# Up-projection sums in PSUM on copies written by ScalarE, a new order of its seven products, and down-projection in halves of 352 columns

## The chip, the cores and the metric

The kernel runs on one core of a Trainium2 chip. Its time is device microseconds, the median of several executions. The core has a matrix engine (TensorE, in the profile PE, with its weight loads as PEld), a vector engine (VectorE, DVE), a scalar engine (ScalarE, ACT), GpSimd (POOL) and SyncE (SP), which here only issues DMA transfers. Matmul results land in PSUM, eight banks of 512 fp32 columns; DVE and ACT read and write PSUM, everything else lies in SBUF.

## The reference

One layer of a streaming encoder for 2048 prompt tokens and 64 sample tokens (2112 columns in all), followed by a final RMSNorm. The part that the change touches is the gated MLP with a causal depthwise convolution of width 3:

```python
h2 = rmsnorm(x, g2) * (1 + sc2) + sh2
up = h2 @ w_up                          # 1024 -> 2 * 2816
upp = jnp.concatenate([conv_buf.astype(up.dtype), up], 1)
conv = b_conv + sum(w_conv[j] * upp[:, j:j + T] for j in range(CONV_W))
a, g = jnp.split(conv, 2, -1)
x = x + gt2 * ((jax.nn.silu(g) * a) @ w_down)   # 2816 -> 1024
```

All inputs and outputs are fp32. Before this part come the adaLN modulation, a pooling mixer, an mLSTM with four heads and the output projection.

## The kernel before

**Precision.** Every large product is made of three passes over operands split into a high and a low part (`PASSES`, L436: high by high, high by low, low by high). ACT writes the high part (L384), DVE the low part (L387); for weights this happens as they come in from memory. A few weights are kept in DRAM already split and are loaded whole.

**The MLP's tiling.** The 2112 tokens are three groups of 704 columns (`FT`), each two halves of 352 (`FH`). The 2816 channels are 22 tiles of 128 (`f`), each with a value tile (a) and a gate tile (g); the pair of both is an object `Pair`. A group is worked in four parts of 5, 5, 6 and 6 pairs (`PARTS`): first the up-projection of the part's pairs, then the down-projection of the part's channels, whose result is added to `x3`.

**Seven products.** For one pair, the two output tiles by two token halves, and the 1024 inputs cut in two, make a 2 by 2 block product, which is done with seven products instead of eight (`product`, L1537: 4 blocks of 128 inputs by 3 passes, 12 matmuls of 352 columns). The names say which sums of the input go in: B11, B21, T2, T3, B22, T1, T4 (`BN`). The weights are two quarters of `w_up`, a third (loaded for T4), and four sums of quarters (`wsum`, made earlier by DVE). The sums of the moving input, tiles `hx`, are made in the order of `BN`: for the first group by ACT and DVE just before the MLP begins (`sums_of`, L728, with L743 and L750), for the others during the group before, through DRAM (`prepare`, `reload`).

The output is put together from the products: the a tile's first half is B11 + B21, its second half B11 + T2 + T1 + B22; the g tile's second half is B11 + T2 + T1 + T3, its first half B11 + T2 + T3 + T4. In `Pair.products` (L1566) PE accumulates in three PSUM banks: b1 takes B11, T2, T1; b2 takes B21 and, after it is read, B22; b3 takes T3 and T4. ACT copies b1 to SBUF after B11 (`s1`, L1582), after T2 (`u2`, L1591) and after T1 (`u4`, L1606), and DVE adds a bank and a copy four times: L1595 for a's first half, and through `plus` (L1551) `sum_a`, `sum_g1`, `sum_g0`. PE's order in a pair is B11, B21, the T4 of the pair before, T2, T3, B22, T1.

**After the sums.** `conv_scale` (ACT, L1525) and two `conv_tap` (DVE, L1530) make the convolution of a and g, `silu` (ACT, L1637) and `gate` (DVE, L1641) the gated value, `split_hi` (ACT, L1646) and `split_lo` (DVE, L1651) its two parts in a tile `av`. These steps are written between the products of the next two pairs.

**Down-projection.** `down` (L1814) multiplies the `av` tiles by `w_down`, for 8 output tiles n; a group of columns (`secs`) has a bank of its own, so one n takes two banks: columns 0 to 448 and 448 to 704 (`ENDS`). The first three n are begun before the last pair is ready, and that pair's remaining steps (`todo`) are done between their matmuls. `down_end` (L1836) adds the banks to `x3` on DVE (L1841). In the last part of the last group the two column groups are worked one after the other, each for n = 3 to 7, so that the output of the first can leave early.

**What sets the order.** In the MLP the kernel's own text is the order of PE, ACT, DVE and POOL (`manual_schedule`); there is no planner between. Each engine takes its instructions in that order. Six PSUM banks go round for `mm_ps()`. The loads are a list, `stream` (L326 to L328 for the up-projection), in the order in which products use them; SP issues them up to seven units ahead (`ahead`, L1493), at most seven weight tiles being live, and the splits of at most four units ahead are written in front of each product (`pump`, L394). Background work (`tick`) of the next group is written between matmuls.

Of the kernel before, what the change touches and what calls it, by code (L numbers as in the profile page):

```python
# [11 lines left out]
AF = mybir.ActivationFunctionType  # L12
ALU = mybir.AluOpType
# [13 lines left out]
FH = FT // 2  # L27
NFG = NTOK // FT
NE = 3
EB = 1  # L30
ENDS = ((0, 448), (448, 704))
PARTS = ((0, 5), (5, 10), (10, 16), (16, 22))
EPS = 1e-6
HD = 128
# [24 lines left out]
def tile_layer(ctx: ExitStack, tc: tile.TileContext, xT, vecs, cst, rst, w_mod, w_ada, w_qkou, w_v, w_pool,  # L59
               w_out, w_up, w_down, st_C, st_pool, yT, o_pool, o_C, o_m, o_conv):  # L60
    nc = tc.nc
    act, dve, pool, pe = nc.scalar, nc.vector, nc.gpsimd, nc.tensor
# [8 lines left out]
    def bank(nm, shape=(P, 512)):  # L71
        q = turn[nm]
        q.append(q.pop(0))
        return q[-1].tile(list(shape), F32, tag="bank", name=nm)
# [3 lines left out]
    def mm_ps():  # L78
        return bank("mm")
# [12 lines left out]
    def scr():  # L92
        return sp.tile([P, TMAX], F32, tag="scr", name="scr")
# [4 lines left out]
    def tick(i=0):  # L98
        q = bg[i]
        while q:  # L100
            try:
                next(q[0])
                return
            except StopIteration:
                q.pop(0)
# [35 lines left out]
    half = cp.tile([P, 8 + 32], F32, tag="half", name="half")[:, :8]  # L141
# [4 lines left out]
    ones_r = cp.tile([P, P], F32R, tag="ones_r", name="ones_r")  # L146
# [102 lines left out]
    for g in range(NG):  # L249
        o = Grp()  # L250
# [20 lines left out]
    stream = []  # L271
# [30 lines left out]
    WS2, WS4, WS3, WS1 = range(4)  # L302
    KEPT = (WS2, WS1)

    def down_order(nf):

        out = [(n, k) for n in range(NE - 1) for k in range(nf - 2)] + [(n, nf - 2) for n in range(NE - 1)]
        out += [(NE - 1, k) for k in range(nf - 1)] + [(n, nf - 1) for n in range(NE)]
        return out + [(n, k) for n in range(NE, KD) for k in range(nf)]

    def up_unit(f, i):
        return w_up[NF + f if i > 1 else f, :, (i % 2) * 512:(i % 2) * 512 + 512]
# [4 lines left out]
    def sum_unit(g, f, i):  # L317
        if i not in KEPT:
            return (wsum[f, :, i], 512, INSIDE, None)
        kept = wsplit[f, KEPT.index(i)]  # L320
        return (kept, 512, WHOLE, None) if g else (wsum[f, :, i], 512, INSIDE, kept)

    for g in range(NFG):
        for (f0, f1_) in PARTS:
            late = []
            for f in range(f0, f1_):  # L326
                stream += [(up_unit(f, 0), 512), (up_unit(f, 1), 512)] + late
                stream += [sum_unit(g, f, i) for i in (WS2, WS3, WS4, WS1)]  # L328
                late = [(up_unit(f, 3), 512)]
            order = down_order(f1_ - f0)  # L330
            ends = g == NFG - 1 and f1_ == NF
            seen = set()
            for i, (n, k) in enumerate(order):
                if i == f1_ - f0 - 2:
                    stream += late
                c = f0 + k // 4 * 4
                if k % 4 == 0 or (n, c) not in seen:
                    seen.add((n, c))
                    d = min(c + 4, f1_)
                    stream.append((w_down[n, :, c * P:d * P], (d - c) * P, OUT, None, ends and n >= NE))  # L340
# [53 lines left out]
    def pump():  # L394

        while True:
            for i, u in enumerate(pend[:ahead[1]]):
                if u.w is not None or live[0] < ahead[2] or u.stays:
                    work_out(u, 2 if i < ahead[1] - ahead[3] else 1)
            if (pos[0] >= len(stream) or len(pend) >= ahead[0] or live[0] >= ahead[2]  # L400
                    or sum(u.w is None for u in pend) >= RB
                    or pos[0] < n_att and sum(u.w is not None for u in pend) >= WB - 2):
                break
            issue()
# [3 lines left out]
    def get_unit():  # L408
        if not pend:
            issue()  # L410
        u = pend.pop(0)
        work_out(u)
        if spare:

            owed.append(u)
        else:
            keep(u)
        return u.w

    def settle(n=0):  # L420
        while len(owed) > n:
            keep(owed.pop(0))
# [203 lines left out]
    for g in range(NFG):  # L626
        o = Grp()
# [6 lines left out]
    B = []  # L634
# [182 lines left out]
    if True:  # L817
# [399 lines left out]
        def proj(o, h):  # L1217
            W = Row()
            ps = [mm_ps() for _ in o.blks]
            gemm(ps, W, h, o)  # L1220
            return ps
# [14 lines left out]
        ends = []  # L1236
# [174 lines left out]
        for o in groups:  # L1411
# [16 lines left out]
            if o.g == 0:  # L1428
                t = scr()
# [11 lines left out]
            for hd in range(NH):  # L1441
# [3 lines left out]
                if o.g == 0 and hd == 0:  # L1445
                    xs = rows_of(groups[1])
                    t = scr()
# [21 lines left out]
            for gi in U_ORDER:  # L1469
                ps = proj(o, h)  # L1470
# [62 lines left out]
    def spans(o, half):  # L1533

        return [(pa, pb, a + 2 + 2 * s) for (i, pa, pb, a, b, s) in o.pieces if i == half]

    def product(ps, Bo, nm, first):  # L1537
        pump()
        settle()
        U = get_unit()  # L1540
        for kc in range(4):
            for pi, (a, b) in enumerate(PASSES):
                pe.matmul(ps[:, :FH], U[:, a, kc * P:(kc + 1) * P], Bo.at(nm, kc, b),  # L1543
                          start=(first and kc == 0 and pi == 0), stop=(kc == 3 and pi == 2), skip_group_check=not first)
            if kc % 2:
                tick(0)
        live[0] -= 1

    def plus(o, half, ext, u, ps):
        for (a, b, d) in spans(o, half):  # L1550
            dve.tensor_tensor(out=ext[:, d:d + b - a], in0=ps[:, a:b], in1=u[:, a:b], op=ALU.add)  # L1551

    def half_tile(nm):
        return f1.tile([P, FH], F32, tag=nm, name=nm)

    class Pair:
# [9 lines left out]
        def products(self, old):  # L1566


            o, Bo, f = self.o, self.Bo, self.f
            self.before = old  # L1570
            older = old and old.before
            b1, b2 = self.b1, self.b4 = mm_ps(), mm_ps()

            def rest(*steps):
                for pair, step in steps:
                    if pair:
                        step(pair)
            rest((old, Pair.copy_u4), (older, Pair.gate))
            product(b1, Bo, "B11", True)
            rest((old, Pair.sum_g1), (old, Pair.sum_a))  # L1580
            self.s1 = half_tile("s1")
            act.activation(self.s1, b1[:, :FH], AF.Copy)  # L1582
            rest((older, Pair.split_hi))
            product(b2, Bo, "B21", True)
            rest((old, Pair.scale_a), (older, Pair.split_lo))
            if old:
                old.last_product()
            rest((old, Pair.taps_a), (old, Pair.sum_g0))
            product(b1, Bo, "T2", False)
            self.u2 = half_tile("u2")  # L1590
            act.activation(self.u2, b1[:, :FH], AF.Copy)  # L1591
            rest((old, Pair.scale_g))
            self.ea = ext_tile(o, f, "a")
            for (a, b, d) in spans(o, 0):
                dve.tensor_tensor(out=self.ea[:, d:d + b - a], in0=b2[:, a:b], in1=self.s1[:, a:b], op=ALU.add)  # L1595
            self.b3 = mm_ps()
            product(self.b3, Bo, "T3", True)
            rest((old, Pair.taps_g))
            tick(1)
            product(self.b4, Bo, "B22", True)  # L1600
            rest((old, Pair.silu))
            product(b1, Bo, "T1", False)

        def copy_u4(self):
            self.u4 = half_tile("u4")
            act.activation(self.u4, self.b1[:, :FH], AF.Copy)  # L1606

        def sum_a(self):
            plus(self.o, 1, self.ea, self.u4, self.b4)

        def scale_a(self):
            self.ta = conv_scale(self.o, self.f, self.ea, "a")

        def sum_g1(self):
            self.eg = ext_tile(self.o, NF + self.f, "g")
            plus(self.o, 1, self.eg, self.u4, self.b3)

        def sum_g0(self):
            plus(self.o, 0, self.eg, self.u2, self.b3)

        def scale_g(self):
            self.tg = conv_scale(self.o, NF + self.f, self.eg, "g")
# [77 lines left out]
    late, YLATE = [], 6  # L1700
# [84 lines left out]
    ET = mybir.EngineType  # L1785
    fctx.enter_context(tc.manual_schedule(engines={ET.PE, ET.Activation, ET.DVE, ET.Pool}))
    x3, ssum = [], None
    for o in fgroups:
        Bo = B[o.g]
        for pi, (f0, f1_) in enumerate(PARTS):  # L1790
            nf = f1_ - f0
            lastp = pi == len(PARTS) - 1
            ends = o.last and lastp
            av = [None] * nf
            pair = None
            for f in range(f0, f1_):
                old, pair = pair, Pair(o, Bo, f, f - f0, av)
# [57 lines left out]
                if ends:  # L1855
                    act.activation(x3[n][:, lo:hi], x3[n][:, lo:hi], AF.Copy, scale=V[:, V_GF + n:V_GF + n + 1])

            both = ENDS
            Ws = [Row() for _ in range(NE)]
            pss = []  # L1860

            old = pair.before
            pair.copy_u4()
            todo.extend([both_of(pair.sum_g1, old.gate), both_of(pair.sum_a, old.split_hi), both_of(old.split_lo, pair.scale_a)])
            for n in range(NE - 1):
                pss.append([mm_ps() for _ in both])
# [14 lines left out]
            rows = {n: Row() for n in range(NE, KD)}  # L1881
            for secs in [(c,) for c in ENDS] if ends else (both,):
                sums = [(ssum, 0)]
                for n in range(NE, KD):
                    ps = [mm_ps() for _ in secs]
# [91 lines left out]
```

## Time and profile before

| | |
|---|---|
| median of 3 runs | 2204.64 us (2204.5 to 2205.43) |
| span of the profiled execution | 2204.2 us |
| PE busy | 2184.3 us, 99% |
| DVE busy | 1572.0 us, 71% |
| ACT busy | 999.1 us, 45% |
| up-projection matmuls (L1543) | 5544 |
| down-projection matmuls (L1823) | 3168 |
| first up-projection matmul | 798.66 us after the span's start |

The page gives no other time of the profiled execution than its span; the median of the runs lies 0.4 us above it. In the rows below, a group is a source line, its engine and operation, "out<-in" by tile names, the shapes and the count; then busy time and the mean of one; then the idle time of the engine just before them and what ended it. In the chain, a piece has its start, its length, its engine, line and count. In the timeline, a piece has its start, its length, engine, line, operation and count, and in brackets the idle time before it.

### The profile page before, as it was taken

What the parts mean: (1) busy time and instruction counts of PE and PEld (TensorE: products, weight loads), DVE (VectorE), ACT (ScalarE), POOL (GpSimd) and SP (SyncE); (2) the same over time, 40 slices, a digit from 0 to 9 for tenths busy, and PEclk for the clock granted to TensorE, in tenths of its full rate; (3) what the DMA queues carried; (4) which work ended last, traced back from release to release, by engine and by line L of the source; (5) the groups of instructions that cost most, each with busy time, mean ns of one, the idle gap of its engine ahead of it and who ended that gap; (6) DMA issues with size and microseconds to landing.
All of it is one profiled execution on the core that took longest, in us unless ns stands there. A gap on an engine that the chain in (4) does not pass through costs nothing.

```text
span 2204.2 us, 37994 instructions
## 1 busy us (share of the span) xinstructions
PE 2184.3 (99%) x13744; PEld 2061.3 (94%) x13744; DVE 1572.0 (71%) x2888; ACT 999.1 (45%) x1981; POOL 196.0 (9%) x474
## 2 busy tenths in 40 slices
PE   8999999999999999999999999999999999999998
PEld 7888888888899999999999999999999999999998
DVE  5867668767855688787858687777767685757475
ACT  4554335334333455464536354545444353445254
POOL 0010000001000100010000210000001210101012
PEclk9999999999999999999999999999999999999999
DMA  8986998998889485747556875565448555353442
GB/s 316 332 292 229 309 301 267 306 298 260 300 256 298 138 272 173 239 167 267 193 182 232 273 273 166 170 207 203 146 162 291 200 172 165 117 173 117 146 151 82
DMA packets 274980, 487.06 MB, mean 221 GB/s; under 512 B 24640, under 2 KB 102976, under 8 KB 274792
## 3 DMA queue, kind: packets, MB, share of 16 engines
q1 hardware_dynamic: 265352, 462.32, 62.9%
q10 hardware_dynamic: 9440, 22.32, 2.6%
q8 instruction: 108, 1.77, 0.3%
q14 instruction: 80, 0.66, 0.1%
HBM read 378.48 MB, written 106.06 MB: 220 GB/s over the span
## 4 chain that ended last, share of the span: by engine, by line
PE 91%; DMA 4%; DVE 2%; issue 1%; SPq 1%; ACT 0%; POOL 0%; POOLq 0%; DVEq 0%; ACTq 0%
PE mm L1543 39%; PE mm L1823 23%; PE mm L450 21%; PE mm L1097 2%; DMA raw<-w_ada 1%; DMA wsum<-w 1%; PE m L1287 1%; PE m L1309 1%; PE m L1307 1%; PE m L1272 1%; DMA wt<-wsum 0%; DMA w<-w_up 0%; DVE s L202 0%; PE mm L1034 0%; DVE scr L242 0%
## 5 line engine op out<-in xcount | busy, mean ns | idle before, releaser
L1543 PE MATMUL mm<-hx,wt 128*128 128x352 f32 x5544 | 883.6, 321 | 2.3 <-ACT s L1582 1.3
L1543 PEld LDWEIGHTS mm<-hx,wt 128*128 128x128 f32 x5544 | 877.5, 188 | 3.2 <-ACT s L1582 1.6
L1823 PE MATMUL mm<-av,wt 128*128 128x448 f32 (+1 forms) x3168 | 510.1, 322 | 0.0
L1823 PEld LDWEIGHTS mm<-av,wt 128*128 128x128 f32 x3168 | 486.2, 188 | 21.8
L384 ACT ACTIVATE wt<-raw 128x512 fp32r<-128x512 f32 (+3 forms) x518 | 286.7, 574 | 227.0 <-PE mm L1823 85.0
L450 PE MATMUL mm<-hl,wt 128*128 128x512 f32 (+2 forms) x1920 | 386.1, 357 | 0.0
L387 DVE TENSOR_TENSOR wt<-raw,wt 128x512 fp32r<-128x512 f32 (+3 forms) x518 | 323.2, 639 | 78.1 <-ACT wt L384 75.8
L450 PEld LDWEIGHTS mm<-hl,wt 128*128 128x128 f32 x1920 | 315.4, 189 | 48.2 <-issue 5.3
L1841 DVE SCALAR_TENSOR_TENSOR x<-mm,MOD,x 128x448 f32<-128x448 f32 (+2 forms) x224 | 111.0, 527 | 117.9 <-PE mm L1823 117.6
L450 PE MATMUL mm<-mx,wt 128*128 128x512 f32 (+1 forms) x960 | 186.7, 356 | 0.0
L450 PEld LDWEIGHTS mm<-mx,wt 128*128 128x128 f32 x960 | 159.7, 188 | 26.1
L1530 DVE SCALAR_TENSOR_TENSOR tg<-eg,V,tg 128x704 f32<-128x704 f32 (+1 forms) x132 | 125.7, 952 | 49.5 <-ACT tg L1525 47.2
L387 DVE TENSOR_TENSOR wt<-wt 128x512 fp32r<-128x512 f32 x176 | 120.5, 686 | 38.2 <-ACT wt L384 38.2
L1530 DVE SCALAR_TENSOR_TENSOR ta<-ea,V,ta 128x704 f32<-128x704 f32 (+1 forms) x132 | 125.6, 952 | 5.3 <-ACT ta L1525 2.9
L384 ACT ACTIVATE wt<-wt 128x512 fp32r<-128x512 f32 x176 | 108.1, 622 | 21.0 <-DMA wt<-wsum 18.6
L1591 ACT ACTIVATE u<-mm 128x352 f32<-128x352 f32 x66 | 30.6, 464 | 159.5 <-PE mm L1543 152.9
L1651 DVE TENSOR_TENSOR av<-tg,av 128x704 fp32r<-128x704 f32 (+1 forms) x88 | 60.5, 708 | 52.4 <-ACT av L1646 52.3
L1551 DVE TENSOR_TENSOR eg<-mm,u 128x352 f32<-128x352 f32 x154 | 70.1, 467 | 36.7 <-ACT u L1606 25.8
L1637 ACT ACTIVATE tg<-tg 128x704 f32<-128x704 f32 (+1 forms) x66 | 52.4, 794 | 78.9 <-DVE tg L1530 78.9
L1582 ACT ACTIVATE s<-mm 128x352 f32<-128x352 f32 x66 | 30.5, 463 | 105.3 <-PE mm L1543 101.1
L1097 PE MATMUL mm<-wt,hl 128*128 128x256 f32 (+1 forms) x576 | 71.3, 284 | 0.0
L1097 PEld LDWEIGHTS mm<-wt,hl 128*128 128x128 f32 x576 | 70.4, 190 | 0.9 <-issue 0.6
(293 smaller groups left out, 1948.7 us busy)
## 6 DMA issues: line engine op xcount, KB each, us to landing
raw<-w_up SPq DMA_DIRECT2D x198, 256.0 KB, 4.0
wt<-hl_kept SPq DMA_DIRECT2D x96, 512.0 KB, 6.2
wt<-wsum SPq DMA_DIRECT2D x176, 256.0 KB, 3.9
wt<-wsplit SPq DMA_DIRECT2D x88, 512.0 KB, 4.6
raw<-w_down SPq DMA_DIRECT2D x96, 256.0 KB, 2.8
w<-w_up SPq DMA_DIRECT2D x88, 256.0 KB, 3.7
wsum<-w SPq DMA_DIRECT2D x44, 512.0 KB, 4.7
wsplit<-wt SPq DMA_DIRECT2D x44, 512.0 KB, 3.6
```

The lines of the kernel that those rows point to most:

```text
L384: act.activation(u.w[:, 0, :u.n], u.raw[:, :u.n], AF.Copy)
L387: dve.tensor_tensor(out=u.w[:, 1, :u.n], in0=u.raw[:, :u.n], in1=u.w[:, 0, :u.n].bitcast(F32), op=ALU.subtract)
L450: pe.matmul(ps[bi][:, :hi - lo], U[:, a, k % 4 * P:(k % 4 + 1) * P], mv[k][:, b, lo:hi], start=(at == 0 and pi == 0), stop=(k == order[-1] ...
L1097: pe.matmul(ps[ti][:n, :cols], h[4 * kh + k4][:, b, lo:lo + n], U[:, a, k4 % 2 * cols:(k4 % 2 + 1) * cols], start=(kh == 0 and k4 == 0 and ...
L1530: dve.scalar_tensor_tensor(out=t[:, :E], in0=ext[:, j:j + E], scalar=wc(j, f), in1=t[:, :E], op0=ALU.mult, op1=ALU.add)
L1543: pe.matmul(ps[:, :FH], U[:, a, kc * P:(kc + 1) * P], Bo.at(nm, kc, b), start=(first and kc == 0 and pi == 0), stop=(kc == 3 and pi == 2), ...
L1551: dve.tensor_tensor(out=ext[:, d:d + b - a], in0=ps[:, a:b], in1=u[:, a:b], op=ALU.add)
L1591: act.activation(self.u2, b1[:, :FH], AF.Copy)
L1637: act.activation(self.tg[:, :E], self.tg[:, :E], AF.Silu)
L1651: dve.tensor_tensor(out=self.d[:, 1, a:b], in0=self.tg[:, a + 2 * s:b + 2 * s], in1=self.d[:, 0, a:b].bitcast(F32), op=ALU.subtract)
L1823: pe.matmul(ps[i][:, :hi - lo], U[:, a, k % 4 * P:(k % 4 + 1) * P], av[k][:, b, lo:hi], start=(k == 0 and (a, b) == PASSES[0]), stop=(k == ...
L1841: dve.scalar_tensor_tensor(out=x3[n][:, a:b], in0=ps[i][:, a - lo:b - lo], scalar=gt2(n, s), in1=x3[n][:, a:b], op0=ALU.mult, op1=ALU.add)
```

## The change

Three things. First, the sums: after B11, ACT copies b1 into b2 (`seed`), still in PSUM, and B21 is added there by PE; after T2, ACT copies b1 into b3, and T3 and T4 are added there; B22 is added to b1. The first product in b3 is T1, which ACT copies to SBUF (`s5`) before b3 is written over. The a and g tiles' first halves are then copies of a bank by ACT (`copied`); their second halves are DVE additions of `s5` and a bank. So there are five ACT copies and two DVE additions for a pair, where there were three and four. Second, the order: PE's products in a pair are B11, T1, the T4 of the pair before, T2, B21, B22, T3, and the loads in `stream` follow; `sums_of` and `BN` keep their order. Third, the down-projection's two column groups are 352 and 352 (`HALVES`), except in the last part of the last group. Six matmuls of 352 columns are put ahead of the first product (`begin_banks`), one for each tile that `mm_ps()` hands out. Their results are not used.

```diff
+HALVES = ((0, 352), (352, 704))
...
-                stream += [(up_unit(f, 0), 512), (up_unit(f, 1), 512)] + late
-                stream += [sum_unit(g, f, i) for i in (WS2, WS3, WS4, WS1)]
+                stream += [(up_unit(f, 0), 512), sum_unit(g, f, WS1)] + late
+                stream += [sum_unit(g, f, WS2), (up_unit(f, 1), 512)] + [sum_unit(g, f, i) for i in (WS4, WS3)]
                 late = [(up_unit(f, 3), 512)]
...
+    def copied(o, half, ext, ps):
+        for (a, b, d) in spans(o, half):
+            act.activation(ext[:, d:d + b - a], ps[:, a:b], AF.Copy)
+
+    def begin_banks():
+
+        for t in [mm_ps() for _ in range(6)]:
+            pe.matmul(t[:, :FH], ones_r, B[-1].at("B11", 0, 0), start=True, stop=True)
+
+    def seed(to, ps):
+
+        act.activation(to[:, :FH], ps[:, :FH], AF.Copy)
...
-            b1, b2 = self.b1, self.b4 = mm_ps(), mm_ps()
+            b1, b2, b3 = self.b1, self.b2, self.b3 = mm_ps(), mm_ps(), mm_ps()
...
-            rest((old, Pair.copy_u4), (older, Pair.gate))
+            rest((older, Pair.gate))
             product(b1, Bo, "B11", True)
             rest((old, Pair.sum_g1), (old, Pair.sum_a))
-            self.s1 = half_tile("s1")
-            act.activation(self.s1, b1[:, :FH], AF.Copy)
+            seed(b2, b1)
             rest((older, Pair.split_hi))
-            product(b2, Bo, "B21", True)
+            product(b3, Bo, "T1", True)
+            self.s5 = half_tile("s5")
+            act.activation(self.s5, b3[:, :FH], AF.Copy)
             rest((old, Pair.scale_a), (older, Pair.split_lo))
             if old:
                 old.last_product()
-            rest((old, Pair.taps_a), (old, Pair.sum_g0))
+            rest((old, Pair.taps_a))
             product(b1, Bo, "T2", False)
-            self.u2 = half_tile("u2")
-            act.activation(self.u2, b1[:, :FH], AF.Copy)
-            rest((old, Pair.scale_g))
+            seed(b3, b1)
+            rest((old, Pair.sum_g0), (old, Pair.scale_g))
             self.ea = ext_tile(o, f, "a")
-            for (a, b, d) in spans(o, 0):
-                dve.tensor_tensor(out=self.ea[:, d:d + b - a], in0=b2[:, a:b], in1=self.s1[:, a:b], op=ALU.add)
-            self.b3 = mm_ps()
-            product(self.b3, Bo, "T3", True)
+            product(b2, Bo, "B21", False)
+            copied(o, 0, self.ea, b2)
             rest((old, Pair.taps_g))
             tick(1)
-            product(self.b4, Bo, "B22", True)
+            product(b1, Bo, "B22", False)
             rest((old, Pair.silu))
-            product(b1, Bo, "T1", False)
+            product(b3, Bo, "T3", False)
 
-        def copy_u4(self):
-            self.u4 = half_tile("u4")
-            act.activation(self.u4, self.b1[:, :FH], AF.Copy)
-
         def sum_a(self):
-            plus(self.o, 1, self.ea, self.u4, self.b4)
+            plus(self.o, 1, self.ea, self.s5, self.b1)
...
-            plus(self.o, 1, self.eg, self.u4, self.b3)
+            plus(self.o, 1, self.eg, self.s5, self.b3)
...
-            plus(self.o, 0, self.eg, self.u2, self.b3)
+            copied(self.o, 0, self.eg, self.b3)
...
+    begin_banks()
     for o in fgroups:
...
-            both = ENDS
+            both = ENDS if ends else HALVES
...
-            pair.copy_u4()
```

## The prediction

> **What bounds the kernel now.** I read the page's engine totals first, then the chain that ended last in order of time, then the idle times and waits of the copies that the change touches, then the timeline of the two places where the new order could be late.
>
> ```profile
> span 2204.2 us, 37994 instructions
> PE 2184.3 (99%) x13744; PEld 2061.3 (94%) x13744; DVE 1572.0 (71%) x2888; ACT 999.1 (45%) x1981; POOL 196.0 (9%) x474
> ...
> L1823 PE MATMUL mm<-av,wt 128*128 128x448 f32 (+1 forms) x3168 | 510.1, 322 | 0.0
> ```
>
> ```profile
> L1543 PE MATMUL mm<-hx,wt 128*128 128x352 f32 x5544 | 883.6, 321 | 2.3 <-ACT s L1582 1.3 <-DVE hx L750 0.9 <-ACT wt L384 0.2
> ```
>
> PE is busy for 99% of the span. The 5544 matmuls of the up-projection (L1543) had 2.3 us of idle time ahead of them in all, the 3168 of the down-projection (L1823) none. So in the part of the program that is changed PE waits for nobody, and what counts is how closely one matmul follows the next. The chain gives that pace: a piece's length over its count.
>
> ```profile
> 1138.78 77.90 PE mm L1543 x492
> 1216.67 3.87 PE mm L1823 x24
> 1222.45 41.99 PE mm L1823 x264
> ...
> 1436.58 2.92 PE mm L1823 x18
> 1441.40 35.45 PE mm L1823 x222
> ```
>
> Up-projection: 77.90/492 = 158.3 ns per 352-column matmul, so a product of 12 takes 1.90 us and seven take 13.3 us. Down-projection, an even mix of 448 and 256 columns: with six tiles in a part (3.87 + 41.99)/288 = 159.2 ns, with five (2.92 + 35.45)/240 = 159.9 ns. The mean width is 352 in both.
>
> **Part 1: sums in PSUM instead of on DVE.** Each of 66 pairs loses two DVE additions (L1595, and sum_g0 at L1551) and gains two ACT copies (three of 352 columns before, five after).
>
> ```profile
> L1551 DVE TENSOR_TENSOR eg<-mm,u 128x352 f32<-128x352 f32 x110 | 57.2, 520 | 24.2 <-ACT u L1606 16.8 <-issue 5.6 <-PE mm L1543 1.7
> L1595 DVE TENSOR_TENSOR ea<-mm,s 128x352 f32<-128x352 f32 x66 | 34.2, 518 | 1.9 <-PE mm L1543 1.8
> L1606 ACT ACTIVATE u<-mm 128x352 f32<-128x352 f32 x66 | 30.7, 464 | 81.6 <-PE mm L1543 81.6
> L1591 ACT ACTIVATE u<-mm 128x352 f32<-128x352 f32 x66 | 30.6, 464 | 159.5 <-PE mm L1543 152.9 <-DVE ea L1595 3.0 <-DVE eg L1551 2.8
> L1582 ACT ACTIVATE s<-mm 128x352 f32<-128x352 f32 x66 | 30.5, 463 | 105.3 <-PE mm L1543 101.1 <-issue 2.2 <-ACT wt L384 1.9
> ```
>
> ```profile
> 1138.00:1217.00 79.00, 79.00 (x502) 78.97 (x501) 60.84 (x91) 44.54 (x77) 6.55 (x20) 1.00 0.66 223
> ```
>
> DVE: -66 x (518 + 520) ns = -68.5 us. ACT: +66 x 2 x 464 ns = +61.2 us. In the stretch 1138 to 1217, of group 0, PE worked 79.00 of 79.00 us, DVE 60.84, ACT 44.54. With 0.93 us per 13.3 us pair added, ACT goes from 56% to 63%; it has room. Neither engine ends a stage, so both terms are 0 on the path: the cover is PE's 13.3 us per pair. A copy that writes PSUM is in no row; I take 464 ns, as for the same read, between half of that and 952 ns (the dearest 704-column row of DVE, a far end); at 952 ns the slack worked out next is still positive.
>
> What is new is that PE waits for ACT closer by. After T2 the copy into b3 must have read b1 before B22 adds to b1, and only B21, 1.90 us, lies between; before, T3 and B22 lay there (3.8 us). The ACT queue ahead of it holds the copy after T1, scale_a, and two weight splits, in the 3.8 us of T4 and T2. The u copy of before (L1591) stands at the same place: after T2, the fourth product. In 61 of 66 pairs it was released by PE.
>
> ```profile
> L1591 ACT ACTIVATE u<-mm x66: 448/464/467, 807.3 to 2138.3; 128x352 f32<-128x352 f32 x66
> ...
>   PE mm L1543: 152.9, 61
>   DVE ea L1595: 3.0, 1
>   DVE eg L1551: 2.8, 2
> ```
>
> ACT sat idle 152.9/61 = 2.5 us ahead of it; the added copy takes 0.46 of that. So the copy ends some 0.5 us after T2 and leaves about 1.4 us to B22. The first copy into b2 has two products to T2 (3.8 us; 1.9 in the first pair of a part, as the s copy has now), sum_g1 now waits for T3 alone and not for a u copy (the 25.8 us of DVE idle there go, off the path), and what the added ACT work makes later, a weight split, is issued four units ahead. All 0. One pair pays:
>
> ```profile
> 915.12 0.63 ACT L384 ACTIVATE wt<-wt 128x512 fp32r<-128x512 f32 x1 [3.95 <-DMA wt<-wsum]
> 915.65 0.45 ACT L1591 ACTIVATE u<-mm 128x352 f32<-128x352 f32 x1
> ...
> 908.09 12.19 PE L1543 MATMUL mm<-hx,wt 128*128 128x352 f32 x76
> ```
>
> Here a split waited 3.95 us for its DMA, and the copy behind it ended at 916.10. T2, the third product (no T4 in a part's first pair), ended at 908.09 + 36 x 0.158 = 913.8, and B21 would end at 915.7: +0.4 us. Such waits number 18 (18.6 us, below): from 0 to a few us. I take +0.4.
>
> **Part 2: the order of products and loads.** The loads follow the products; the kept pre-split units (512 KB) move from fourth and seventh to second and fourth. No DMA is added. SP issues them six to seven units ahead, PE has been idle 0.2 us in all for splits, and that is the cover: 0. The other place is the start. The moving sums hx are still made in the order B11, B21, T2, T3, B22, T1, T4, and T1 becomes PE's second product.
>
> ```profile
> 798.66 1.75 PE L1543 MATMUL mm<-hx,wt 128*128 128x352 f32 x10
> 801.31 2.50 PE L1543 MATMUL mm<-hx,wt 128*128 128x352 f32 x14 [0.89 <-DVE hx L750]
> 805.09 5.18 PE L1543 MATMUL mm<-hx,wt 128*128 128x352 f32 x31 [1.29 <-ACT s L1582]
> ...
> 805.43 0.52 DVE L750 TENSOR_TENSOR hx<-fscr,hx 128x352 fp32r<-128x352 f32 x1
> 805.87 0.68 DVE L387 TENSOR_TENSOR wt<-wt 128x512 fp32r<-128x512 f32 x1
> 806.47 0.95 DVE L750 TENSOR_TENSOR hx<-fscr,hx 128x352 fp32r<-128x352 f32 x2
> ...
> 804.60 0.44 ACT L1582 ACTIVATE s<-mm 128x352 f32<-128x352 f32 x1
> ```
>
> The two at 806.47 are the low parts of T1 and T4. In the built program the weight split at 805.87 comes behind T1's, so T1's is done at about 806.4; two matmuls wait for it, T1 ends at 806.4 + 2 x 0.16 = 806.8, and T2 starts then instead of at 805.09 (where it waited for the s copy): +1.7 us. Ends: 0, if T1's part comes before the copy as it would without the DVE queue, and +2.9, if the six matmuls of begin_banks (6 x 0.16 = 1.0, and 0.2 for the waits among them) add fully. They stand ahead of B11, which waits for hx until 801.31 anyway: 0.
>
> **Part 3: halves of 352.** The last part of group 2 keeps 448/256, so 3168 - 288 = 2880 matmuls change. Now they take 5 x 45.86 + 6 x 38.37 = 459.5 us. At the 158.3 ns of the up-projection, the same width: 455.9, -3.6 us. At no change: 0. Against it:
>
> ```profile
> 448.92 13.21 PE L450 MATMUL mm<-hl,wt 128*128 128x512 f32 x57
> ...
> 352.99 44.96 PE L450 MATMUL mm<-mx,wt 128*128 128x512 f32 x192
> ```
>
> The same 512 columns, taken from two operand tiles, cost (13.21 - 0.40)/56 = 228.8 and (44.96 - 0.40)/191 = 233.3 ns (0.40 is one matmul's own time): where the operand lies is worth up to 4.5 ns. The halves read av, at another offset than hx. With that surcharge on 158.3: 162.8 x 2880 = 468.9, +9.4 us. I take 158.7, between the 158.3 of this width and the 159.05 of av's long runs (41.99/264): 457.1 us, -2.4 us. The evictions stay:
>
> ```profile
> L1841 DVE SCALAR_TENSOR_TENSOR x<-mm,MOD,x 128x448 f32<-128x448 f32 x96 | 65.2, 679 | 61.3 <-PE mm L1823 60.9
> L1841 DVE SCALAR_TENSOR_TENSOR x<-mm,MOD,x 128x256 f32<-128x256 f32 x64 | 30.7, 479 | 35.6 <-PE mm L1823 35.6
> ```
>
> Two of (679 + 479)/2 = 579 ns instead of 679 + 479, behind the next row's matmuls: 0.
>
> The Trainium skill (TensorE: Matmul & The Clock Gate, section Back-to-back issue gap) puts the isolated gap at N/2.4 + 2.5 ns, a straight line in N. By that rule two halves cost what 448 + 256 cost, the term is 0 and the sum 2206.7; the trace does not agree in the level (the rule gives 149 ns for 352 columns, the rows 158.3), and so I do not take its slope either.
>
> **Sum.** The span is 2204.2 us; the median of the runs, 2204.64, lies 0.4 above it. 2204.64 + 0.4 + 1.7 - 2.4 = 2204.3 us. A measurement here tells about 0.2% (4.4 us) from no change: this is no change.
>
> **Rivals.**
> (1) Slower by the operand's place: each half costs the 4.5 ns more. 2204.64 + 0.4 + 1.7 + 9.4 = 2216.1 us. For it: the two L450 rows. Against it: av's own runs of 448 and 256 average 159.05, close to hx's pace. It decides from (4.4 - 2.1 + 3.6)/2880 = 2.0 ns on.
> (2) Slower by a late copy: ACT takes its queue in order, and a split ahead of a copy waits for its DMA.
>
> ```profile
> ACT wt L384 <- DMA wt<-wsum: 18.6, 18, 3.9
> ```
>
> If each of these 18 waits stands ahead of a copy into b3 and the slack of 1.4 us covers only a third of it, about 12 us reach PE instead of 0.4: 2204.64 + 12 + 1.7 - 2.4 = 2215.9. Against it: one such case in 66 pairs now.
> (3) It does not do what it says for the time: DVE's 68.5 us are worth nothing, as above, and neither are the halves (0 in place of -2.4): 2206.7 us, still no change.
> (4) Faster by over 0.2%: the start free (0), halves at 158.3 (-3.6), the few stalls of L1543 gone (-2.3): 2204.64 - 5.9 = 2198.7. All three must hold.
>
> **How the numbers follow.** Forecast with (3), 2201 to 2208: 0.72. Rival 1: 0.09. Rival 2: 0.12, of which half lies above 2211. Rival 4: 0.06. 0.01 is left over, slower. So faster 0.06, same 0.72, slower 0.22. For 8 in 10 the range takes in the forecast and the lower part of rivals 1 and 2: 2200.8 to 2212; the forecast's own range is 2201 to 2208.
>
> **What would show it.** Right: L1543's idle time stays near 3 us, with T2 of the first pair the largest; a 288-matmul down stage takes about 45.7 us; DVE loses some 68 us, ACT gains 61, and the span does not follow. Wrong: idle time of PE behind an ACT copy in most pairs (the 1.4 us of slack were wrong), or a down stage over 46.5 us (the operand's place), or one much under 45.6.

## The result, and the profile after

The changed kernel takes 2208.74 us (median of 20 runs), the kernel before, on the same chip, 2205.63 us: a ratio of 1.0016, with a 95% interval of 1.0009 to 1.0022. It is slower by 3.1 us by the medians and by 3.5 us by the ratio, where 2204.3 us and no change were forecast. Of the 4.4 us between the forecast and the measured time, 1.0 us lies in the kernel before, which took 2205.63 us here and 2204.64 us in the runs from which the forecast started. In the profiled executions the span went from 2204.2 to 2206.5 us.

The page's totals and the two groups of the MLP's matmuls, after (line 1543 of before is now 1544, line 1823 is 1832):

```profile
span 2206.5 us, 38048 instructions
PE 2188.6 (99%) x13750; PEld 2085.7 (95%) x13750; DVE 1515.5 (69%) x2756; ACT 1053.3 (48%) x2113; POOL 213.1 (10%) x474
...
L1544 PE MATMUL mm<-hx,wt 128*128 128x352 f32 x5544 | 884.8, 321 | 1.4 <-DVE hx L751 1.4
...
L1832 PE MATMUL mm<-av,wt 128*128 128x352 f32 (+2 forms) x3168 | 511.8, 323 | 0.0
```

DVE lost 56.5 us, ACT gained 54.2, and the idle time ahead of the up-projection fell from 2.3 to 1.4 us. None of that made PE wait more, and PE is still 99% busy. What grew is the busy time of the down-projection's group, which has no idle time at all: its matmuls follow each other more slowly. The chain that ended last, after, shows it stage by stage:

```profile
1096.36 42.25 PE mm L1832 x264
1138.61 77.90 PE mm L1544 x492
1216.52 3.87 PE mm L1832 x24
1222.38 42.25 PE mm L1832 x264
...
1437.33 2.90 PE mm L1832 x18
1442.23 35.53 PE mm L1832 x222
```

The up stage is 77.90 us, to the hundredth what it was. The down pieces are (3.87 + 42.25)/288 = 160.1 ns per matmul for six tiles, where they were 159.2, and (2.90 + 35.53)/240 = 160.1 for five, where they were 159.9.

In the experiments below, a down stage runs from the start of its first matmul to the start of its last, with the last product T4 between them. By that count a stage of five tiles went from 40.15 to 40.27 us, one of six from 47.64 to 47.96; the last part, which keeps 448 and 256 columns, stayed at 50.59. Over all stages the down-projection grew by 2.15 us. The last matmul of a stage lies outside that count, and the halves widen it from 256 to 352 columns: from its start to the next up stage, the eleven stages together took 1.28 us before and 1.76 us after. So the halves cost 2.63 us in the traces. The up-projection shrank by 0.66 us, its start moved by -0.13, and the end after the last matmul grew by 0.5: with the 2.63, the 2.3 us between the two spans. The 0.5 us do not belong to the change: from the start of the last down matmul to the end, the halves alone took 9.83 us, as before, and the kernel before with wider `av` tiles (below) took 10.32, nearly the 10.33 of after. The ratio's interval reaches from 2.0 to 4.9 us.

### The profile page after: what moved, and what is told of

It is laid out like the page before. It is cut to its first block, busy times and chain, and to the rows that moved or that the text cites. A ratio compares the mean times of both kernels' runs of the same rounds, so it can differ in the third digit from the quotient of the medians.

```text
span 2206.5 us, 38048 instructions
## 1 busy us (share of the span) xinstructions
PE 2188.6 (99%) x13750; PEld 2085.7 (95%) x13750; DVE 1515.5 (69%) x2756; ACT 1053.3 (48%) x2113; POOL 213.1 (10%) x474
## 4 chain that ended last, share of the span: by engine, by line
PE 91%; DMA 4%; DVE 3%; issue 1%; ACT 1%; SPq 0%; POOL 0%; POOLq 0%; DVEq 0%; ACTq 0%
PE mm L1544 40%; PE mm L1832 23%; PE mm L451 20%; PE mm L1098 1%; DMA raw<-w_ada 1%; DMA wsum<-w 1%; PE m L1288 1%; PE m L1310 1%; PE m L1308 1%; DVE scr L243 1%; PE m L1273 1%; DVE wt L388 0%; DVE s L203 0%; PE mm L1035 0%; PE m L1263 0%
## 5 line engine op out<-in xcount | busy, mean ns | idle before, releaser
L1544 PE MATMUL mm<-hx,wt 128*128 128x352 f32 x5544 | 884.8, 321 | 1.4 <-DVE hx L751 1.4
L1544 PEld LDWEIGHTS mm<-hx,wt 128*128 128x128 f32 x5544 | 879.5, 188 | 2.3 <-DVE hx L751 1.7
L1832 PE MATMUL mm<-av,wt 128*128 128x352 f32 (+2 forms) x3168 | 511.8, 323 | 0.0
L1832 PEld LDWEIGHTS mm<-av,wt 128*128 128x128 f32 x3168 | 506.1, 188 | 2.0
L1850 DVE SCALAR_TENSOR_TENSOR x<-mm,MOD,x 128x352 f32<-128x352 f32 (+4 forms) x224 | 111.2, 526 | 136.4 <-PE mm L1832 136.4
L1565 ACT ACTIVATE mm<-mm 128x352 f32<-128x352 f32 x132 | 59.1, 448 | 232.9 <-PE mm L1544 228.1
L1649 DVE TENSOR_TENSOR tg<-ta,tg 128x704 f32<-128x704 f32 (+1 forms) x66 | 58.7, 890 | 16.1 <-ACT tg L1645 16.1
L1526 ACT ACTIVATE tg<-eg,V 128x704 f32<-128x704 f32 (+1 forms) x66 | 64.6, 978 | 3.3
```

The lines of the kernel that those rows point to most:

```text
L1526: act.activation(t[:, :E], ext[:, 2:2 + E], AF.Identity, scale=wc(2, f), bias=V[:, V_BC + f:V_BC + f + 1])
L1565: act.activation(to[:, :FH], ps[:, :FH], AF.Copy)
L1649: dve.tensor_tensor(out=self.tg[:, :E], in0=self.ta[:, :E], in1=self.tg[:, :E], op=ALU.mult)
L1832: pe.matmul(ps[i][:, :hi - lo], U[:, a, k % 4 * P:(k % 4 + 1) * P], av[k][:, b, lo:hi], start=(k == 0 and (a, b) == PASSES[0]), stop=(k == ...
L1850: dve.scalar_tensor_tensor(out=x3[n][:, a:b], in0=ps[i][:, a - lo:b - lo], scalar=gt2(n, s), in1=x3[n][:, a:b], op0=ALU.mult, op1=ALU.add)
```

## The experiments

Ratios are to the kernel before, on the same chip, with 95% intervals.

**One part alone.** The halves on the kernel before:

```diff
+HALVES = ((0, 352), (352, 704))
-            both = ENDS
+            both = ENDS if ends else HALVES
```

> The kernel before with only the down-projection's column groups changed to 352 and 352 (the last part of the last group keeps 448 and 256). Theory A (the loss is the pace of the 352-column matmuls on av, 160.0 ns in the changed kernel against a mean of 159.2 to 159.9 before): the down stage of a six-tile part goes from 47.64 to 47.96 us, of a five-tile part from 40.15 to 40.27 us, in all about +2.2 us in the stages, ratio 1.001; the up-projection stages stay (64.60 and 77.90 us). Theory B (the loss comes from the new sums and order, through copies that are late or through the start): no change in the time, ratio 1.000, and the down stages do not account for the loss. Theory C (the halves gain only where the ACT copies leave PE alone): down stages under 47.64 us here.

And the changed kernel with its halves undone:

```diff
-            both = ENDS if ends else HALVES
+            both = ENDS
```

> The changed kernel with the old column groups 448 and 256 everywhere. The sums of the up-projection are wrong in columns 256 to 351 of some banks, since the 256-column matmuls leave those columns unmarked; the instructions and their number are those of the changed sums and order, so the time is that of part 1 and part 2 alone. Theory A: down stages back at 47.64 and 40.15 us, the whole between 0.5 us less and 1.5 us more than before, ratio 0.9998 to 1.0007. Theory B: the loss stays, ratio 1.0010 to 1.0020.

Measured: halves alone 1.0010 (1.0001 to 1.0019), sums and order alone 0.9999 (0.9990 to 1.0007). The chain of the halves alone, and then that of the sums alone:

```profile
1013.11 79.61 PE mm L1544 x492
...
1098.59 42.25 PE mm L1824 x264
1140.84 77.90 PE mm L1544 x492
```

```profile
1218.57 3.87 PE mm L1832 x24
1224.35 41.99 PE mm L1832 x264
```

The 42.25 us comes with the halves and goes with them. So the loss of the down stages lies in the halves, at 160.0 to 160.2 ns from start to start, and the new sums and their order show no loss in the medians. What the second expectation says of wrong columns concerns values, not time, and no run here isolates it. One up stage of the first kernel took 79.61 us with no idle time in it; that comes back below.

**The operand's place, first try.** In the built program, up-projection's operands all begin 128 bytes past a multiple of 256 (`HX, HO = 2 * 384, 32`), the two halves of `av` at 160 and 32. The first try gave each plane of `av` 16 words more, in the kernel after and in the kernel before, so that nothing begins off a multiple of 64 bytes; but 720 words a plane also means that the place changes from buffer to buffer (0, 64, 128 and 192).

```diff
-            self.d = f2.tile([P, 2, FT], F32R, tag="av", name="av", bufs=6)
+            self.d = f2.tile([P, 2, 720], F32R, tag="av", name="av", bufs=6)[:, :, 8:8 + FT]
```

> The changed kernel with each av tile 16 columns wider per part and its data moved by 8 columns, so that both halves of both parts begin at a multiple of 64 bytes, as hx does, instead of 32 bytes past one. Theory A1 (the place of the operand's first byte sets the pace): the down matmuls of 352 columns go from 160.0 to 158.3 ns, a six-tile stage from 47.96 to about 47.5 us, 2880 matmuls give 4.8 us, ratio to the kernel before about 0.9995. If only one of the four places to which the tiles now fall (0, 64, 128, 192 modulo 256) is fast, a part of that. Theory A2 (the pace belongs to the down-projection's stream, not to the place): 160.0 ns and 47.96 us as in the changed kernel, ratio 1.0016.

> The kernel before, columns 448 and 256, with the same widening of av. Theory A1: the 448-column matmuls, at 200 ns and after a change of width 205 to 208 ns, lose up to 1.7 ns each, the down stages (47.64 us, 40.15 us) 0.2 to 0.5 us each, in all 2 to 5 us, ratio 0.998 to 0.999. Theory A2: no change, 47.64 us and ratio 1.000.

Measured: 1.0087 (1.0074 to 1.0100) and 1.0054 (1.0042 to 1.0066), both slower. The chain of the first and of the second:

```profile
1096.91 42.63 PE mm L1832 x264
1139.54 81.98 PE mm L1544 x492
```

```profile
906.72 68.00 PE mm L1543 x408
...
1224.82 42.29 PE mm L1823 x264
```

The place matters, but not as a multiple of 64 bytes: the down pieces grew, most with the halves (42.25 to 42.63). And whole up stages, whose code and operands were not touched, ran at 81.98/492 = 166.6 ns from their first matmul to their last (68.00/408 = 166.7 in the second), three stages in each kernel. The theory as it was put fell.

**The same place in all buffers.** The next three keep the place from buffer to buffer. The tile is made 64 words longer and its contents are shifted:

```diff
-            self.d = f2.tile([P, 2, FT], F32R, tag="av", name="av", bufs=6)
+            self.d = f2.tile([P, 1472], F32R, tag="av", name="av", bufs=6)[:, 56:56 + 2 * FT].rearrange("p (a t) -> p a t", a=2)
```

With 56 words the halves of the kernel after begin at 128 and 0:

> The kernel after, with each of down-projection's input tiles given 64 words more and its two planes moved by 56 words, so that every operand of a half begins at 128 or 0 bytes past a multiple of 256 (up-projection's operands all begin at 128; now the halves begin at 160 and 32), and the same in all six buffers. Theory C, the pace of 352 columns is set by this place when it is kept from matmul to matmul: the halves run at up-projection's 158.3 ns instead of 160.0 to 160.2, so the stage of five tiles takes 39.85 us instead of 40.27 and that of six 47.46 instead of 47.96; 11 stages give 5.0 us, about 2203.7 us, 0.9991 of before. Theory D, the second matrix's own order of matmuls sets 160.0 ns wherever the operand lies: 40.27 and 47.96 us as in after, 1.0015 of before. Between them if only one of the two halves gains: 1.000 to 1.0005.

With 40 in place of 56, at 64 and 192:

> The same with a shift of 40 words: the halves begin at 64 and 192 bytes past a multiple of 256, in all six buffers. Where places were mixed from buffer to buffer, matmuls at 64 took 160.2 ns and those at 192 took 161.1 ns, and whole up stages fell to 166.6 ns. Theory C1 (a place has its own price): 40.3 to 40.5 us and 48.0 to 48.3 us, some 1.0015 to 1.003 of before, and slow up stages only if the place left by the last half is what starts them. Theory C2 (the mixing was the cost, any fixed place is as good as another): 158.3 to 160.2 ns, at most 40.27 and 47.96 us, no slow up stage, 0.999 to 1.0015.

And with 56 in the kernel before, both of its parts begin at 128:

> The kernel before (448 and 256 columns) with that shift of 56 words: both parts begin at 128. Theory C: in the mixed run 448 columns at 128 took 198.6 ns and 256 columns 117.5 ns against 201.4 and 117.7 ns at 160; if that holds with the place kept, 1584 pairs gain 3.0 ns each, 4.8 us: about 0.998 of before, down stages 39.8 and 47.2 us. Theory D: no change, 1.000, 40.15 and 47.64 us. The third case, a new phase that slows whole up stages as in the mixed run (3.4 or 4.1 us each): above 1.001.

Measured: 1.0000 (0.9991 to 1.0009), 1.0061 (1.0049 to 1.0074) and 1.0122 (1.0108 to 1.0135). The chains in that order:

```profile
976.84 2.88 PE mm L1832 x18
981.62 35.32 PE mm L1832 x222
...
1094.84 3.81 PE mm L1832 x24
1100.55 42.08 PE mm L1832 x264
1142.63 77.90 PE mm L1544 x492
```

```profile
1097.11 42.23 PE mm L1832 x264
1139.34 81.98 PE mm L1544 x492
```

```profile
1016.23 82.00 PE mm L1543 x492
...
1230.30 42.64 PE mm L1823 x264
```

In the first, the half at 128 ran at 158.4 to 158.7 ns and the half at 0 at 159.9 to 160.8, in the same stages, one after the other; that is the case between the two theories. In the second, the halves at 64 and 192 ran at 159.8 to 160.2 ns, the old pace, so most of the 42.63 above came from the mixing; the ratio is above the figures of both theories, by three up stages at 81.98 us, 12 us in all. The third refutes the carry-over to other widths: 448 columns at 128 took 203.4 to 203.9 ns, more than the 201.4 at 160; and six up stages were slow. The 198.6 of the mixed kernel, on which the expectation rests, was that of its stages of six tiles; in its stages of five, 448 columns at 128 took 203.1 ns, so 198.6 did not belong to the place alone. The place that is the best of those tried for 352 columns is worse than 160 for 448.

**Both halves at 128, and the converse.** Now the four halves of a tile (two planes, two halves) lie 384 words apart instead of 352, so that all begin at 128; the last part of the last group stays as it was:

```diff
+            t = f2.tile([P, 1600], F32R, tag="av", name="av", bufs=6)[:, 56:56 + 4 * 384]
+                d = t.rearrange("p (a h t) -> p a h t", a=2, h=2)[:, :, :, :FH]
...
-                        pe.matmul(ps[i][:, :hi - lo], U[:, a, k % 4 * P:(k % 4 + 1) * P], av[k][:, b, lo:hi],
+                        pe.matmul(ps[i][:, :hi - lo], U[:, a, k % 4 * P:(k % 4 + 1) * P], av[k](b, lo, hi),
```

> The kernel after, with the four halves of each of down-projection's input tiles (two planes, two halves) 384 words apart in place of 352, so that each half begins 128 bytes past a multiple of 256, as up-projection's operands do; the last part of the last group keeps 448 and 256 columns at 160. With one half at 128 and the other at 0, the half at 128 took 158.4 to 158.7 ns and the half at 0 159.9 to 160.8 ns. Theory C (the place sets the pace of 352 columns, and both halves now have the place of up-projection's operands): 158.3 ns for both, 39.75 us for a down stage of five tiles and 47.38 us for one of six; against 40.27 and 47.96 in after that is 6.0 us over 11 stages, about 0.999 of before, up stages at 64.60 and 77.90. Theory D (a change of half in the middle of a tile row costs the phase, wherever the halves lie): one of the halves stays near 160 ns, 39.94 and 47.65 us, about 1.000. Third case, up stages at 166.6 ns: above 1.002.

The converse leaves `av` alone and moves up-projection's operands, in the kernel before, from 128 to 32:

```diff
-HX, HO = 2 * 384, 32
+HX, HO = 2 * 384, 8
```

> The converse, on the kernel before: up-projection's operands (352 columns each, in tiles with 32 words of room ahead) begin 32 bytes past a multiple of 256 instead of 128, by 8 words of room in place of 32; nothing else. The second half of down-projection's columns lies at 32 in after and takes 160.2 ns. Theory C (the place sets the pace): up's matmuls go from 158.35 to about 160.2 ns, stages from 64.60 to 65.35 us and from 77.90 to 78.8 us, 10 us over 5544 matmuls, 1.0046 of before. Theory D (the pace belongs to the second matrix's matmuls, not to the place): 64.60 and 77.90 us, 1.000. Third case, the slow pace of 166.6 ns: 68.0 and 82.0 us, up to 1.02.

Measured: 0.9988 (0.9979 to 0.9997) and 1.0043 (1.0031 to 1.0056). The chain of the halves at 128:

```profile
1138.99 77.90 PE mm L1544 x492
1216.89 3.80 PE mm L1842 x24
1222.59 41.80 PE mm L1842 x264
```

and of the converse:

```profile
1140.35 78.72 PE mm L1543 x492
1219.07 3.83 PE mm L1823 x24
1224.83 41.97 PE mm L1823 x264
```

The halves at 128 run at (3.80 + 41.80)/288 = 158.3 ns, up-projection's own pace, with 39.74 us for a stage of five (39.75 expected) and 47.34 for one of six (47.38 expected). In the converse, up-projection's matmuls, the same instructions on the same data, go to 78.72/492 = 160.0 ns, the pace of the halves, and the down stages hardly move (40.10 and 47.61). So the place of the moving operand sets this pace, in either matrix: by 1.5 to 2.5 ns at 352 columns between 128 and the other five places that were kept through a kernel (0, 32, 64, 160, 192).

**The start.** PE's timeline at the start of the MLP, after:

```profile
797.40 1.29 PE L1561 MATMUL mm<-hx,ones_r 128*128 128x352 f32 x6
798.53 3.92 PE L1544 MATMUL mm<-hx,wt 128*128 128x352 f32 x22
803.90 9.14 PE L1544 MATMUL mm<-hx,wt 128*128 128x352 f32 x56 [1.44 <-DVE hx L751]
```

T1, the second product, waits 1.44 us for its low part. When the sums `hx` come differs from trace to trace, so the start is best read from them. The last low part of B11 on DVE, before, and the same and that of T1 (the second of the two), after:

```profile
800.73 0.52 DVE L750 TENSOR_TENSOR hx<-fscr,hx 128x352 fp32r<-128x352 f32 x1
```

```profile
798.20 0.52 DVE L751 TENSOR_TENSOR hx<-fscr,hx 128x352 fp32r<-128x352 f32 x1
...
802.89 0.95 DVE L751 TENSOR_TENSOR hx<-fscr,hx 128x352 fp32r<-128x352 f32 x2
```

T2, the third product, began at 805.09 us before and at 804.32 us after, which is 3.84 and 5.60 us after the end of B11's last low part (801.25 and 798.72). All five traces with the old order of products give 3.84 or 3.85 us, and all six with the new order and the sums in their old order give 5.60 or 5.61.

The remedy is to make the sums of the input in the order in which the products want them; `BN` and all else stay. It was tried on the sums alone (448 and 256 columns) and on the halves at 128:

```diff
         dve.tensor_tensor(out=t2, in0=b22, in1=t1, op=ALU.subtract)
-        parts(("B21", b21))
+        parts(("T1", t1))
...
-        parts(("T3", t3))
+        parts(("B21", b21))
...
-        parts(("T1", t1))
+        parts(("T3", t3))
```

> The new product order with 448 and 256 columns in down-projection, and the combinations of the normalised input made in the order in which the products now want them: B11, T1, T2, B21, B22, T3, T4 (T1 and B21 moved). If the wait of 1.4 us for T1's low part at the start holds the end, the first stage begins its pace that much earlier: 0.9993 of before, and no idle time by VectorE's hx ahead of the up products. If what precedes it sets the start (the first product came at 797.5 to 801.6 us in five traces of the same code ahead), the wait only moves: 0.9999 as without the reorder.

> The same, with the combinations of the input also made in the order in which the products want them (B11, T1, T2, B21, B22, T3, T4). The sums with 448 and 256 columns went from 0.9999 to 0.9987 of before by that order, and their first stage from 67.45 to 66.50 us; if the two edits add, this takes 1.0 to 2.6 us less than the one without it: 0.998 of before. If the wait for T1's low part is no longer there to win once the phases differ: the same as without.

Measured: 0.9987 (0.9978 to 0.9996) and 0.9976 (0.9967 to 0.9985). The timeline of the first, and the chain and the group of the second:

```profile
797.76 1.29 PE L1561 MATMUL mm<-hx,ones_r 128*128 128x352 f32 x6
798.89 13.22 PE L1544 MATMUL mm<-hx,wt 128*128 128x352 f32 x78
```

```profile
1215.14 3.80 PE mm L1842 x24
1220.84 41.80 PE mm L1842 x264
```

```profile
L1544 PE MATMUL mm<-hx,wt 128*128 128x352 f32 x5544 | 883.6, 321 | 0.0
```

The wait is gone, all 5544 matmuls run without a gap ahead of them, and the first up stage falls from 67.45 to 66.50 us in the one and from 68.11 to 66.49 in the other. T2 begins 3.91 and 3.92 us after B11's last low part, 1.7 us sooner than without the edit. By the medians the edit is worth 0.12% (2.6 us) in both, more than the traces show, but the intervals with and without it overlap in both. The last kernel, the change with its halves at 128 and its input sums in order, takes 2201.2 us beside 2206.56 of before: 0.24% less, where the kernel after took 0.16% more.

## Why the prediction was wrong

**The pace of the halves: the step that failed.** Part 3 took 158.7 ns for 352 columns out of `av`, between two paces measured elsewhere, and so -2.4 us. They run at 160.1, and the down stages became longer, by 2.63 us with the last matmul of each. By the chain's pieces, which the prediction added up, they took 5 x 46.12 + 6 x 38.43 = 461.2 us instead of 459.5. That term alone is off by 4 to 5 us, more than the whole loss. The step assumed that the pace lies between that of the same width in another tile and that of the same tile at other widths. It lies outside, because a pace belongs to a width at a place (the stages at 166.6 ns, below, apart). The kernel with the halves at 128 shows both sides of the error: there the pieces give 5 x (3.80 + 41.80) + 6 x (2.85 + 35.15) = 456.0 us, a term of -3.5, close to the lower end of -3.6, and it is 1.8 ns per matmul that turns it round.

**Rival 1 had the mechanism, not the size.** "Slower by the operand's place" is what happened, with 1.8 ns over 158.3 per matmul in place of 4.5. The point from which it was said to decide, 2.0 ns, was nearly reached, and it was reached by being near the old pace: 448 and 256 columns at their old place average 159.6, so even 160.1 costs only 2 to 3 us. The two rows from which its 4.5 ns came do differ in place (`hl` at 0, `mx` at 224 bytes past a multiple of 256 in the built program), but at 512 columns, and no run tests whether the place makes their difference. The rival was given 0.09 because `av`'s own long runs stood close to hx's pace; those were runs of other widths, and the kernel before with both parts at 128 showed how little one width says of another.

The Trainium skill (TensorE: Matmul & The Clock Gate, section Back-to-back issue gap) gives an isolated gap that hangs on the width alone. In the streams of these runs the width alone does not set the spacing: the same 352 columns took 158.3, 160.0 and 166.6 ns.

**The sums: right.** The 68.5 and 61.2 us of the prediction were 56.5 and 54.2 in the page, and the span did not follow them: the sums alone are 0.9999 of before. (The page counts overlapping instructions once; added one by one, the additions on DVE lost 68.7 us and the copies on ACT gained 58.1.) A copy that writes PSUM took a little less than one into SBUF; the wait view of the new copies, after:

```profile
L1565 ACT ACTIVATE mm<-mm x132: 441/448/450, 802.1 to 2140.2; 128x352 f32<-128x352 f32 x132
...
  PE mm L1544: 228.1, 121
```

It shows 448 ns, against the 464 taken. ACT waited for PE ahead of 121 of the 132 copies, with 1.9 us a time, so the slack held, and rival 2 did not happen.

**The late copy: +0.4, measured 0.** The second up stage of group 0, where it was expected, took 64.60 us as before.

**The start: +1.7, and right by the traces.** The first up stage went from 68.53 to 67.78 us, which looks like a gain of 0.75. But the two traces differ in when `hx` came: B11's last low part ended 2.53 us earlier after than before. Against it T2 began 1.76 us later, as forecast, and T1's low part came before the weight split, as the prediction had read. Over all traces B11's last low part ended at 799.5 to 801.3 us with the old order of products and at 798.7 to 803.6 with the new one, so nothing shows that the change moved it: an earlier `hx` hid the cost in this pair of traces. With the 2.63 us of the halves the 1.76 make 4.4 us, inside the 2.0 to 4.9 of the ratio's interval; alone they would be 1.0008, just above the interval of the sums alone, so the medians do not confirm their size. Of three terms, then, one failed and one held; the late copy did not happen.

**Rival 4, by another kernel.** The halves at 128 with the sums in order meet its three conditions: the start is free, the halves run at 158.3 ns, and L1544 has no idle time. It was worked out at -5.9 us; that kernel measured -5.4 (2206.56 to 2201.2 us).

**What stays open.** Why the place acts as it does is not settled, nor what sends whole up stages to 166.6 ns. Such stages came only in kernels whose `av` places or column groups were changed, at the same parts in each group, and the slow pace held from the first matmul to the last. The converse kernel, with hx at 32, had none. The single 79.61 us stage of the halves alone was in one group only, and there the pace changed in the middle. Two stretches of that stage in the chain:

```profile
1014.86 43.22 PE mm L1544 x273
...
1062.89 29.17 PE mm L1544 x175
```

The first 300 matmuls ran at 158.3 ns (43.22/273); then two intervals of 195 and 243 ns followed, and the rest ran at 166.7 ns (29.17/175). All of them have their moving operands at 128. So the same matmuls at the same place can run at either pace, and the 166.6 ns are not the price of their own place; what starts them, and how a neighbouring stage's places bear on it, no run here shows.

## What to carry to other kernels

Where PE is 99% busy with no idle time ahead of a group, the spacing of matmuls is the bound, and it belongs to a width at a place: after a change of widths or tiles, take the pace from the chain (piece over count) for each group, and try the places that the tile's padding allows before judging the widths. Check the untouched stages as well, since their pace can change with the neighbours'. And when the start of a stage is compared between two traces, measure it from the end of the work that it waits for, since that work itself moved by up to 5 us from trace to trace here.

## What was not expected of the hardware

- A matmul of 352 columns followed the last after 158.3 ns when its operand began 128 bytes past a multiple of 256, and after 159.8 to 160.8 ns at 0, 32, 64, 160 and 192, kept through the kernel. For 448 columns, 128 was the worse place: 203.4 to 203.9 ns against 201.4 at 160.
- Where the place changed from tile to tile, 352 columns cost more on average than at any one place kept: 161.4 ns in a stage of six tiles, (3.85 + 42.63)/288. At 0 it was up to 166.6 ns there, against 159.9 to 160.8 when the place was kept.
- Stages whose own code and operands had not changed ran 5.2% slower throughout (81.98 against 77.90 us, 68.00 against 64.60), at the same granted clock (0.998), after a change of the stages beside them: three of them in three kernels and six in a fourth. In one more kernel a stage went from 158.3 to 166.7 ns in its middle, with its operands at the same place throughout.
